# Splits of the last feed-forward operands as steps behind the first products, three weight adds on the Vector engine, and the tail's product on GpSimd

## The chip, the cores and the metric

The kernel runs on one core of a Trainium2 chip. The metric is the device time of one execution in microseconds, and the comparison is between medians of several runs. The kernel before took 2356.03 us (median of three: 2354.13, 2356.03 and 2356.07). The profile is of one further execution, which took 2354.07 us.

The engines go by the names of the profile: PE is the Tensor engine, which multiplies matrices, DVE the Vector engine, ACT the Scalar engine, POOL is GpSimd and SP the engine whose queue issues nearly all DMA transfers. Each engine works through its own list of instructions strictly in order, and waits at an instruction until what it needs is there.

## The reference

One layer of a trunk over x of 2048 rows by 1024, and a last norm. The part that the change touches begins at the output projection:

```python
x = x + merged @ w_out[l]
xn = rms_norm(x, ffn_norm_g[l])
gate, up = jnp.split(xn @ w_gate_up[l], 2, axis=-1)
x = x + (jax.nn.silu(gate) * up) @ w_down[l]
return rms_norm(x, final_norm_g)
```

with `rms_norm(x, g) = x * rsqrt(mean(x*x) + EPS) * g`. D_MODEL is 1024 and D_FF 2816. Everything ahead of that (attention with forget gates, spatial gating, their norms) fills `merged` and is the same in both kernels.

## The kernel before

**Precision.** Every float32 operand of a product is split in two: a high part rounded to the matrix format (a CAST on ACT, line 127) and the remainder, low (a subtraction on DVE, line 130). A product is three passes: high by high, high by low, low by high. So each operand of a product costs one ACT and one DVE instruction of its size before PE may use it.

**The output projection** (products at line 1190) goes row block by row block of 128 rows. When both halves of a block are added to x (line 1184, on DVE, reading the products' banks), `out_done` finishes it: ACT squares the row and sums it (1157), DVE makes mean plus EPS (`r3a`, 174), POOL takes the inverse root as a power (`r3r`, 177, in the helper `rsqrt`), DVE scales the row (`xn`, 1163), PE transposes it (1170), ACT copies the transposed tiles out (1172) and SP stores them in the DRAM buffer XT. The feed-forward reads its operand from XT.

**The feed-forward** computes each block product from 7 products of halves instead of 8, with sums and differences of the operands' quarters. The resident operand, from XT, has quarters b11, b12, b21, b22 in four large tiles `sg` (each 128 partitions by 4 by 512, so 128x2048). From these `first_operands` makes the seven resident operands of the first set: R4 = b22 - b12, R1 = t1 = b11 + b12, R3 = b22 - t1, R0 = b11, R2 = b21, R5 = b21 - t1, R6 = b22, each as a high and a low half. It is a generator, and the out-projection's loop takes steps of it in between. R5 and R6 are the last step, taken ahead of the feed-forward's loop. The subtraction for R5 is done on the whole tile, after the sum b11 + b12 has been made a second time over b11. `keep_as` writes the high and low half of an operand over tiles that are free.

The streamed operand is a weight. An `Up` item is 128 columns of gate and the same of up; its four quarters (`raw`, each 128x512) are loaded by `load` at line 1520 and combined by `stream`, which yields the seven operands one by one, each with its split `wh`, `wl`. There are four sums or differences among them. Which engine does each is read from the string `SE = 'pvpv'` (p is POOL, v DVE), through the helper `tt` at line 1433. The first, a21 + a22, is on POOL.

There are 22 Up items for each half of the rows (sets 1 and 2), then three sets of 8 `Down` items. Two items make a group, and a group has seven slots, n = 0 to 6. In the loop over slots PE multiplies the slot's operands (1743), then `evac` takes the result out of its bank: `u` is ACT's copy of the slot 0 product (1535 in Up, 1490 in Down), and the other slots add to it. The loop also calls `make`, which asks `stream` for operands some slots ahead. Each set's resident operands are made by `refill` during the last group of the set before, one in each slot.

**The tail.** The last Down item holds the last two row blocks. In its `evac` at slots 3 and 4 a half row's squares are summed (1594) and the half is multiplied by the final norm's gain (1583 and 1590, both on DVE). In `done`, when the other half is there too, it is squared, the sums joined (1605), POOL takes the root (1607), DVE scales one half by root and gain (1609) and ACT the one that has the gain already by the root alone (1611). All four halves are stored by SP (1610 and 1612).

**What sets the order.** A framework's scheduler places every instruction on its engine's list, mostly in the order of the program, with priorities and the buffers' reuse. So moving a step in the program moves instructions in each list, and the lists have to be read to see where.

Of the kernel before, what the change touches and what calls it, by code (L numbers as in the profile page):

```python
# [11 lines left out]
ALU = mybir.AluOpType  # L12
# [13 lines left out]
CH = 512  # L26
# [58 lines left out]
def trunk(ctx: ExitStack, tc: tile.TileContext, x, x_t, mix_g, w_in, b_f, ln_g, ln_b, w_st, b_st, on_g, w_out,  # L85
# [1361 lines left out]
                sg.append(fetch(s, n + 4))  # L1447
            yield r

    def stream(a11, a12, a21, a22):  # L1450

        kh = a11.shape[1]

        tt(SE[0], a21, a21, a22, ALU.add)
        yield split(a11, kh)
        tt(SE[1], a11, a21, a11, ALU.subtract)
        yield split(a11, kh)
        yield split(a12, kh)
        tt(SE[2], a12, a12, a11, ALU.subtract)
        tt(SE[3], a11, a22, a11, ALU.subtract)  # L1460
        yield split(a21, kh)
        yield split(a11, kh)
        yield split(a22, kh)
        yield split(a12, kh)
# [44 lines left out]
    class Up:  # L1509
# [12 lines left out]
            self.raw = raw  # L1522

        def start(self):
            self.ops = stream(*self.raw)

        def evac(self, n):
            ps = self.ps
# [27 lines left out]
    class Down(Rows):  # L1556
# [10 lines left out]
            self.raw = raw  # L1567

        def start(self):
            self.ops = stream(*self.raw)  # L1570

        def source(self, t):
            return XA[t]
# [1 line left out]
        def evac(self, n):  # L1575
            super().evac(n)
            if (self.kb, self.tp, n) == (2, NB // 2 - 1, 3):

                xt = self.x[0][:, 0:CH]
                self.a = T(pev, [P, 1], F32, "a5")  # L1580
                self.squares(xt, self.a)
                nc.vector.tensor_scalar(self.a, self.a, 1.0 / D, EPS, ALU.mult, ALU.add)
                nc.vector.tensor_tensor(xt, xt, finb[:, 0:CH], ALU.mult)
            if (self.kb, self.tp, n) == (2, NB // 2 - 1, 4):

                xt = self.x[1][:, CH:]
                self.b = T(pev, [P, 1], F32, "b5")
                self.squares(xt, self.b)
                nc.vector.tensor_scalar(self.b, self.b, 1.0 / D, EPS, ALU.mult, ALU.add)
                nc.vector.tensor_tensor(xt, xt, finb[:, CH:], ALU.mult)  # L1590

        def squares(self, xt, ss):
            jk = T(pev, [P, D], mybir.dt.bfloat16, "jk", bufs=1)
# [2 lines left out]
        def done(self, t, xt, at):  # L1596
            if self.kb < 2:
                ld(XA[t], xt)
                return
            ss = T(pev, [P, 1], F32, "ss4")  # L1600
            o = out[t * P : (t + 1) * P, :]
            if t >= NB - 2:
                at, by, c = (slice(CH, D), slice(0, CH), self.a) if t == NB - 2 else (slice(0, CH), slice(CH, D), self.b)
                self.squares(xt[:, at], ss)
                self.last = nc.vector.scalar_tensor_tensor(ss, ss, 1.0 / D, c, ALU.mult, ALU.add)
                r = T(pev, [P, 1], F32, "r4r")
                nc.gpsimd.tensor_tensor(r, ss, mhalf[:, 0:1], ALU.pow)
                yield
                nc.vector.scalar_tensor_tensor(xt[:, at], xt[:, at], r, finb[:, at], ALU.mult, ALU.mult)
                ld(o[:, at], xt[:, at])  # L1610
                nc.scalar.activation(xt[:, by], xt[:, by], AF.Copy, scale=r)
                ld(o[:, by], xt[:, by])
                return
            while now[0] == at:
                yield
            with behind(*copies):
                self.squares(xt, ss)
            yield
            r = rsqrt(pev, ss, 1.0 / D, "r4")
            nc.vector.scalar_tensor_tensor(xt, xt, r, finb, ALU.mult, ALU.mult)  # L1620
            ld(o, xt)
            yield
# [43 lines left out]
    def first_operands():  # L1666
# [2 lines left out]
        for i in range(4):  # L1669
            yield  # L1670

        def halves(a, src, t=None, add=None):
            R[a] = resident(a)
            for i in range(2):
                o = slice(2 * i, 2 * i + 2)
                u = t[i] if t else src[:, o]
                if add:
                    tt("v", u, add[0][:, o] if add[0] is not t else u, add[1][:, o] if add[1] is not t else u, add[2])
                hi_of(nc.scalar, R[a][0][:, o], u)
                yield  # L1680
                lo_of(nc.vector, R[a][1][:, o], u, R[a][0][:, o])
                yield

        yield from halves(4, b12, add=(b22, b12, ALU.subtract))
        t1 = [raw4().rearrange("p (a b) t -> p a (b t)", a=2) for _ in range(2)]
        yield from halves(1, None, t1, (b11, b12, ALU.add))
        yield from halves(3, None, t1, (b22, t1, ALU.subtract))
        yield "wait"
        R[0] = keep_as(0, b11)
        R[2] = keep_as(2, b21)  # L1690
        yield "wait"
        with behind(E["sq"], E["xn"]):
            tt("v", b11, b11, b12, ALU.add)
            tt("v", b21, b21, b11, ALU.subtract)
            R[5] = keep_as(5, b21)
            R[6] = keep_as(6, b22)
        yield "wait"

    fo = first_operands()
    m, at = 0, None  # L1700
    for _ in og:
# [3 lines left out]
        if E["t"] == NB - 2 and E["half"] == 0 and not loaded:  # L1705
# [2 lines left out]
            next(fo)  # L1708
            load(0)
            make()  # L1710
    next(fo)
    make()
    load(1)
    nextR = [None] * 7
# [2 lines left out]
    for q in range(len(slots)):  # L1717
# [9 lines left out]
        last = last and s < 5  # L1727
        if n == 0 and last:
            fill = refill(s + 1, sg)
        while nq < len(slots) and len(made) + len(grp[slots[nq][0]][2]) <= LW:  # L1730
            make()
        if n == 0:
# [16 lines left out]
        for m in () if late and n == 0 else (0, 1) if late and n == 1 else (n,):  # L1749
            for it in its:  # L1750
                it.evac(m)
        if n == 0:
            now[0] = p
        tail = p == len(grp) - 1
# [4 lines left out]
        if tail and n == 6:  # L1759
            next(posts[1])  # L1760
            with behind(its[0].last):
                next(posts.pop(0), None)
        if last:
            nextR[n] = next(fill)
        if sums and p:
            try:
                sums.send((n, p))
# [48 lines left out]
```

## Time and profile before

| What | us |
|---|---|
| median of three runs | 2356.03 |
| the profiled execution | 2354.07 |
| its span, first to last instruction | 2352.4 |
| PE busy in the span | 2325.9 (99%) |
| DVE, ACT, POOL busy | 1681.5, 1059.0, 607.6 |
| PE waiting for xn (line 1163), three times | 4.1 |
| PE waiting for a weight's low half (130) in the feed-forward, twice | 1.7 |
| PE waiting for the copy u, in Up and in Down, once each | 1.0 and 1.0 |

The span starts with the first instruction and times in it are counted from there; 1.7 us of the execution lie outside it. PE works without pause but for short waits, so whatever time the kernel can lose or gain shows as a gap between two of PE's instructions or as time after its last one. The out-projection ends and the feed-forward begins at about 1077 us, the down projection begins at about 1900 us, and PE's last product ends at about 2343 us.

### The profile page before, as it was taken

To read this page: it belongs to the slowest core of one execution; us is meant where nothing else is said; L and a number is where in the kernel's file an instruction comes from. 1 tells how busy PE (TensorE), PEld (TensorE's weight loads), DVE (VectorE), ACT (ScalarE), POOL (GpSimd) and SP (SyncE) were. 2 spreads that over 40 slices of the span, in tenths; PEclk is the share of its full clock that TensorE was granted. 3 is DMA by queue.
4 is the path that set the end of the run, shared out by engine and by line. 5 is a ranking of instruction groups with operands and counts; after the bars stand their busy time and mean duration, and the time that the engine had idled before them with its cause. 6 is when DMAs were issued, how large, how long until landed. Compare 5 with 4: busy or idle time off the path is not lost.

```text
span 2352.4 us, 31826 instructions
## 1 busy us (share of the span) xinstructions
PE 2325.9 (99%) x10566; PEld 1889.8 (80%) x10566; DVE 1681.5 (71%) x2783; ACT 1059.0 (45%) x1774; POOL 607.6 (26%) x704
## 2 busy tenths in 40 slices
PE   9999999999999999999999999999999999999998
PEld 7778777777787778877888888888888878888886
DVE  6658668888888677576565666866666686685788
ACT  5322137767788786344323233532333352332433
POOL 1100011121121232131222323232323235343431
PEclk9999999999999999999999999999999999999999
DMA  8845668656677785773445444724444355564554
GB/s 270 296 158 190 210 185 213 179 160 174 175 216 245 223 244 163 230 225 117 125 126 176 139 150 127 241 76 140 129 140 144 90 196 190 191 250 170 194 193 150
DMA packets 375948, 423.90 MB, mean 180 GB/s; under 512 B 23956, under 2 KB 277588, under 8 KB 371816
## 3 DMA queue, kind: packets, MB, share of 16 engines
q1 hardware_dynamic: 359800, 378.62, 52.2%
q0 software_dynamic: 7616, 27.33, 3.4%
q10 hardware_dynamic: 8368, 15.91, 1.9%
q8 instruction: 85, 1.39, 0.3%
q14 instruction: 79, 0.65, 0.1%
HBM read 280.87 MB, written 140.91 MB: 179 GB/s over the span
## 4 chain that ended last, share of the span: by engine, by line
PE 72%; DVE 4%; DMA 2%; issue 2%; ACT 1%; POOL 0%; SPq 0%; POOLq 0%; DVEq 0%; ACTq 0%
PE pp L1743 51%; PE z L930 5%; PE pp L1190 2%; PE oz L1190 2%; PE tp L774 2%; PE tp L769 2%; PE mx_ps L737 2%; PE mx_ps L736 2%; PE tp L771 1%; PE mx_ps L361 1%; DVE wl L130 1%; PE z L971 1%; DVE raw L1433 0%; DMA sg<-XT 0%; DVE Pl L130 0%
## 5 line engine op out<-in xcount | busy, mean ns | idle before, releaser
L127 ACT CAST wh<-raw 128x512 fp32r<-128x512 f32 (+2 forms) x492 | 304.5, 621 | 741.1 <-PE pp L1743 640.6
L130 DVE TENSOR_TENSOR wl<-raw,wh 128x512 fp32r<-128x512 f32 (+2 forms) x496 | 370.9, 755 | 26.9 <-ACT wh L127 26.7
L1743 PE MATMUL pp<-wl,wh 128*128 128x512 f32 x1056 | 325.5, 389 | 2.1 <-ACT u L1535 1.0
L1743 PE MATMUL pp<-wh,wh 128*128 128x512 f32 x1056 | 325.2, 389 | 0.0
L1433 POOL TENSOR_TENSOR raw<-raw 128x512 f32<-128x512 f32 (+1 forms) x124 | 170.5, 1376 | 572.8 <-DMA raw<-in_w_gu_dram 311.2
L130 DVE TENSOR_TENSOR Pl<-Pt,Ph 128x512 fp32r<-128x512 f32 (+1 forms) x320 | 194.3, 614 | 75.3 <-ACT Ph L127 68.4
L1743 PEld LDWEIGHTS pp<-wl,wh 128*128 128x128 f32 x1056 | 198.0, 188 | 44.4 <-ACT u L1535 1.4
L1743 PEld LDWEIGHTS pp<-wh,wh 128*128 128x128 f32 x1056 | 198.1, 188 | 41.2
L739 ACT ACTIVATE Pt<-mx_ps 128x512 f32<-128x512 f32 (+1 forms) x320 | 168.7, 533 | 113.4 <-PE mx_ps L737 94.8
L1743 PE MATMUL pp<-wh,wl 128*128 128x512 f32 x528 | 205.4, 389 | 0.0
L1743 PE MATMUL pp<-wl,wl 128*128 128x512 f32 x528 | 205.4, 389 | 0.0
L1433 DVE TENSOR_TENSOR raw<-raw,raw 128x512 f32<-128x512 f32 (+1 forms) x112 | 136.5, 1219 | 90.2 <-POOL raw L1433 87.4
L930 PE MATMUL z<-wh,xz 128*128 128x512 f32 x496 | 187.3, 396 | 0.0
L127 ACT CAST Ph<-Pt 128x512 fp32r<-128x512 f32 (+1 forms) x320 | 175.7, 557 | 14.6 <-DMA ST<-zvh 0.9
L363 DVE TENSOR_REDUCE mx<-mx_ps 128x1 f32<-128x512 f32 x192 | 130.3, 684 | 19.9 <-PE mx_ps L361 19.0
L749 POOL TENSOR_SCALAR_AFFINE_SELECT Ph<-Ph 128x128 fp32r<-128x128 f32 x128 | 49.7, 388 | 293.8 <-DVE Pl L130 200.8
L361 PE MATMUL mx_ps<-D,A 66*128 66x512 f32 (+2 forms) x320 | 118.5, 374 | 2.6 <-DVE mx L366 1.6
L736 PE MATMUL mx_ps<-A,D 74*128 74x512 f32 (+1 forms) x320 | 117.9, 369 | 0.8 <-ACT Pt L739 0.7
L774 PE MATMUL tp<-Pl,V 128*128 128x512 f32 (+1 forms) x320 | 117.6, 368 | 0.8 <-POOL Pl L749 0.3
L769 PE MATMUL tp<-Ph,V 128*128 128x512 f32 (+1 forms) x320 | 117.2, 366 | 0.6 <-POOL Ph L749 0.5
L737 PE MATMUL mx_ps<-B,C 128*128 128x512 f32 (+1 forms) x320 | 117.3, 367 | 0.0
L1743 PEld LDWEIGHTS pp<-wl,wl 128*128 128x128 f32 x528 | 99.1, 188 | 20.6
(354 smaller groups left out, 5281.4 us busy)
## 6 DMA issues: line engine op xcount, KB each, us to landing
raw<-in_w_gu_dram SPq DMA_DIRECT2D x88, 512.0 KB
xz<-XS SPq DMA_DIRECT2D x31, 1024.0 KB
HD<-hT SPq DMA_DIRECT2D x44, 512.0 KB
SM<-xa SPq DMA_DIRECT2D x30, 512.0 KB
D<-KH SPq DMA_DIRECT2D x112, 128.0 KB
XA<-xa SPq DMA_DIRECT2D x27, 512.0 KB
sg<-SM SPq DMA_DIRECT2D x12, 1024.0 KB
raw<-HD SPq DMA_DIRECT2D x24, 512.0 KB
```

What stands on the lines that cost most here:

```text
L127: return nc.scalar.copy(o, i) if eng is nc.scalar else eng.tensor_copy(o, i)
L130: return eng.tensor_tensor(o, i, f(h), ALU.subtract)
L361: last_mx.append(nc.tensor.matmul(pm[:, 0:n], lhs, Dt[0 : lhs.shape[0], 0:n], start=True, stop=True))
L363: nc.vector.tensor_reduce(mx[:, a, s : s + 1], pm, AX.X, ALU.max)
L736: nc.tensor.matmul(st[:, off:], Dt[:, b * P : (b + 1) * P], A[:, off:], start=True, stop=False)
L737: nc.tensor.matmul(st[:, off:], C[:, b * P : (b + 1) * P], B[:, off:], start=False, stop=True)
L739: nc.scalar.activation(Pt[:, off:], st[:, off:], AF.Exp)
L769: nc.tensor.matmul(pv[:, off:], V[:, 0:P], Ph[:, off:], start=kb == 0, stop=False)
L774: nc.tensor.matmul(pv[:, off:], V[:, 0:P], Pl[:, off:], start=False, stop=kb == 4 * j + 3)
L930: nc.tensor.matmul(pz, xz[a][:, k, :], w[b][:, k, :], start=n == 0, stop=n == 3 * KT - 1)
L1433: return (nc.vector if e == "v" else nc.gpsimd).tensor_tensor(o, a, b, op)
L1743: nc.tensor.matmul(pm, a[:, k, :], b[:, k, :], start=on is None and k == 0 and e == 0, stop=k == it.kh - 1 and e == 2, skip_group_check=n ...
```

## The change

The change has four parts.

First, in Up items of the first half with fi below 2, the sum a21 + a22 is done on DVE and not on POOL.

Second, the source of R5 is made half by half together with R1: `halves` takes a new argument, and while t1's half is in hand it also does b12 = b21 - t1 for that half (128x1024 each). So b11 + b12 is not made a second time. The splits of R5 and R6 become two steps, taken in the feed-forward's loop after the products of slots 1 and 2 of the first group.

Third, for the set that follows the second Up set, the steps for R5 and R6 are taken at slots 0 and 2 of the new set's first group and not in the last group of the old one.

Fourth, in the tail, the multiplication by the gain at line 1590 is done on POOL, and the stores at line 1612 are issued by ACT.

```diff
-    def stream(a11, a12, a21, a22):
+    def stream(a11, a12, a21, a22, e="p"):
         kh = a11.shape[1]
-        tt(SE[0], a21, a21, a22, ALU.add)
+        tt(e, a21, a21, a22, ALU.add)
         yield split(a11, kh)
...
         def start(self):
-            self.ops = stream(*self.raw)
+            self.ops = stream(*self.raw, "v" if not self.half and self.fi < 2 else SE[0])
...
         def start(self):
-            self.ops = stream(*self.raw)
+            self.ops = stream(*self.raw, SE[0])
...
                 nc.vector.tensor_scalar(self.b, self.b, 1.0 / D, EPS, ALU.mult, ALU.add)
-                nc.vector.tensor_tensor(xt, xt, finb[:, CH:], ALU.mult)
+                nc.gpsimd.tensor_tensor(xt, xt, finb[:, CH:], ALU.mult)
...
                 nc.scalar.activation(xt[:, by], xt[:, by], AF.Copy, scale=r)
-                ld(o[:, by], xt[:, by])
+                nc.scalar.dma_start(o[:, by], xt[:, by])
...
-        def halves(a, src, t=None, add=None):
+        def halves(a, src, t=None, add=None, rest=None):
...
                 lo_of(nc.vector, R[a][1][:, o], u, R[a][0][:, o])
+                if rest:
+                    tt("v", rest[0][:, o], rest[1][:, o], u, ALU.subtract)
                 yield
...
-        yield from halves(1, None, t1, (b11, b12, ALU.add))
+        yield from halves(1, None, t1, (b11, b12, ALU.add), (b12, b21))
...
-        with behind(E["sq"], E["xn"]):
-            tt("v", b11, b11, b12, ALU.add)
-            tt("v", b21, b21, b11, ALU.subtract)
-            R[5] = keep_as(5, b21)
-            R[6] = keep_as(6, b22)
-        yield "wait"
+        for i, src in ((5, b12), (6, b22)):
+            with behind(E["sq"], E["xn"]):
+                R[i] = keep_as(i, src)
+            yield "wait"
...
-    next(fo)
     make()
     load(1)
...
+            over = [5, 6] if s == 2 else []
...
+        if p == 0 and n in (1, 2):
+            next(fo)
...
-        if last:
+        if last and n not in over:
             nextR[n] = next(fill)
+        if s == 3 and i == 0 and n in (0, 2):
+            R[over.pop(0)] = next(fill)
```

Three places show how the lists move. A row is line, operation, output<-inputs and the tile's size; the numbers in the names tell buffers apart and differ a little between the two kernels.

**POOL, at the end of the out-projection, before.** `raw_3186` and `raw_12165` are the sums a21 + a22 of the first two Up items, `r3r` and `rar` roots of rows, `rd` row sums.

```order
L177 TENSOR_TENSOR rar_11876<-raa_11874,mhalf_206 128x1
L1433 TENSOR_TENSOR raw_3186_12161<-raw_3186_12161 128x512
L177 TENSOR_TENSOR r3r_11859<-r3a_11857,mhalf_206 128x1
L1100 TENSOR_TENSOR rd_11842<-rd_11842 128x256
L1101 TENSOR_TENSOR rd_11842<-rd_11842 128x128
L1433 TENSOR_TENSOR raw_12165<-raw_12165 128x512
L177 TENSOR_TENSOR r3r_11981<-r3a_11979,mhalf_206 128x1
```

The same piece of DVE in the changed kernel; `R3l` is the low half of R3, `wl` a weight's low half, `xn` a scaled row.

```order
L174 TENSOR_SCALAR raa_11875<-tp_11862 128x1
L130 TENSOR_TENSOR R3l_11941<-raw_3104_11775,R3h_11940 128x1024
L174 TENSOR_SCALAR r3a_11858<-ss_3119_11834 128x1
L1184 SCALAR_TENSOR_TENSOR xa_11674<-pp_11848,rsg_208,xa_11674 128x512
L1163 SCALAR_TENSOR_TENSOR xn_11833<-xb_11562,r3r_11860,ffb_10117 128x1024
L1184 SCALAR_TENSOR_TENSOR xa_11674<-pp_11870,rar_11877,xa_11674 128x512
L130 TENSOR_TENSOR R3l_11941<-raw_11776,R3h_11940 128x1024
L1094 TENSOR_TENSOR raw_3122_11842<-raw_3122_11842,rd_11843 128x512
L1184 SCALAR_TENSOR_TENSOR xa_11674<-pp_11891,rsg_208,xa_11674 128x512
L130 TENSOR_TENSOR wl_11960<-raw_11836,wh_11959 128x512
L1433 TENSOR_TENSOR raw_3186_12163<-raw_3186_12163 128x512
```

```order
L1184 SCALAR_TENSOR_TENSOR xa_11674<-pp_11917,rar_11877,xa_11674 128x512
L130 TENSOR_TENSOR wl_11964<-raw_3122_11842,wh_11963 128x512
L1433 TENSOR_TENSOR raw_12167<-raw_12167 128x512
L174 TENSOR_SCALAR r3a_11981<-ss_3150_11969 128x1
L174 TENSOR_SCALAR raa_11997<-tp_11986 128x1
L1163 SCALAR_TENSOR_TENSOR xn_11968<-xa_11674,r3r_11983,ffb_10117 128x1024
```

Both sums are on DVE, the first behind the row's scaling, the second just ahead of the next row's r3a; on POOL the roots follow each other. Both halves of R3's low part, which stood together ahead of the first of these rows, now stand around it.

**DVE, where the feed-forward begins.** Before; the tiles of 128x2048 belong to R5 and R6.

```order
L1163 SCALAR_TENSOR_TENSOR xb_12247<-xa_11913,r3r_12252,ffb_10117 128x1024
L1433 TENSOR_TENSOR sg_3047_11504<-sg_3047_11504,sg_3048_11505 128x2048
L130 TENSOR_TENSOR wl_12260<-sg_3050_11507,wl_12260 128x2048
L1433 TENSOR_TENSOR sg_3049_11506<-sg_3049_11506,sg_3047_11504 128x2048
L130 TENSOR_TENSOR wl_12326<-raw_3186_12161,wh_12325 128x512
L130 TENSOR_TENSOR wl_12332<-raw_12165,wh_12331 128x512
L130 TENSOR_TENSOR wl_12392<-raw_3185_12159,wh_12391 128x512
L130 TENSOR_TENSOR wl_12396<-raw_12163,wh_12395 128x512
L130 TENSOR_TENSOR wh_12257<-sg_3049_11506,wh_12257 128x2048
```

And in the changed kernel:

```order
L1163 SCALAR_TENSOR_TENSOR xb_12249<-xa_11915,r3r_12254,ffb_10117 128x1024
L130 TENSOR_TENSOR wl_12320<-raw_3186_12163,wh_12319 128x512
L130 TENSOR_TENSOR wh_12385<-sg_3048_11505,wh_12385 128x2048
L130 TENSOR_TENSOR wl_12326<-raw_12167,wh_12325 128x512
L130 TENSOR_TENSOR wl_12422<-sg_3050_11507,wl_12422 128x2048
L130 TENSOR_TENSOR wl_12389<-raw_3185_12161,wh_12388 128x512
L130 TENSOR_TENSOR wl_12393<-raw_12165,wh_12392 128x512
```

Two of the four large pieces are left, and a weight's low half stands ahead of each. On ACT at the same place the two copies u stood behind two casts of the next weights, and now behind one. From the loop's second group to the tail the lists of all engines are the same in both kernels.

**DVE and ACT in the tail.** DVE in the changed kernel, where the row of line 1590 stood between the first two rows before:

```order
L1589 TENSOR_SCALAR b_4974_22084<-b_4974_22084 128x1
L1433 TENSOR_TENSOR sg_4955_22001<-sg_4955_22001,u_22004 128x512
L1505 TENSOR_TENSOR sg_4955_22001<-sg_4955_22001,pp_22056 128x512
L1605 SCALAR_TENSOR_TENSOR ss_4977_22101<-ss_4977_22101,b_4974_22084 128x1
L1605 SCALAR_TENSOR_TENSOR ss_4980_22117<-ss_4980_22117,a_4971_22067 128x1
```

ACT in the changed kernel, whose list ended before with the second of the two rows of line 1611:

```order
L1594 ACTIVATE jk_22102,ss_4977_22101<-sg_4955_22001 128x512
L1594 ACTIVATE jk_22118,ss_4980_22117<-sg_4955_22001 128x512
L1611 ACTIVATE sg_4955_22001<-sg_4955_22001,r4r_22105 128x512
L1611 ACTIVATE sg_4955_22001<-sg_4955_22001,r4r_22121 128x512
L1612 DMA out_dram<-sg_4955_22001 128x512 x2
```

Both stores of line 1612 come after both scalings on ACT's list; before, SP issued them, the first of them ahead of the two stores of line 1610.

## The prediction

> **What bounds the kernel now.** I read the page first, then all waits of TensorE (PE), then the timeline around each of PE's gaps. A timeline row is start (us), length (us), engine, line, operation, output<-inputs, and in brackets the idle time before it and what ended that.
>
> ```profile
> PE 2325.9 (99%) x10566; PEld 1889.8 (80%) x10566; DVE 1681.5 (71%) x2783; ACT 1059.0 (45%) x1774; POOL 607.6 (26%) x704
> PE tp L1170 <- DVE xn L1163: 4.1, 3, 2.2
> PE pp L1743 <- DVE wl L130: 1.7, 2, 0.9
> PE pp L1743 <- ACT u L1535: 1.0, 1, 1.0
> PE pp L1743 <- ACT u L1490: 1.0, 1, 1.0
> ```
>
> PE is busy 99% of the span, so only its gaps can be saved, plus the tail after its last product. The wait rows give the total, the count and the longest. Of those on xn one stands ahead of everything that changes, the others at 1039.31 and 1080.38 (both shown below); those on wl at 1093.33 (below, 0.93) and in the down projection (the rest of the 1.7, 0.78), those on u at 1099.59 and in the down projection (0.97). Nothing else that PE waits for lies in code that the diff touches. So the sum has four places: the rows' roots, the start of the feed-forward, the start of the down projection, the tail.
>
> **Part 1, the rows' roots.** Both out-projection rows' chains at the first place, before:
>
> ```profile
> 1030.78 2.42 DVE L130 TENSOR_TENSOR R3l<-raw,R3h 128x1024 fp32r<-128x1024 f32 x2
> 1033.12 0.74 DVE L1184 SCALAR_TENSOR_TENSOR xb<-pp,rar,xb 128x512 f32<-128x512 f32 x1
> 1033.90 1.06 ACT L1157 ACTIVATE xn<-xb 128x1024 f32<-128x1024 f32 x1 [0.95 <-DVE xb L1184]
> 1035.11 0.14 DVE L174 TENSOR_SCALAR r3a<-ss 128x1 f32<-128x1 f32 x1
> 1036.04 1.29 POOL L1433 TENSOR_TENSOR raw<-raw 128x512 f32<-128x512 f32 x1 [0.89 <-DMA raw<-in_w_gu_dram]
> 1037.29 0.55 POOL L177 TENSOR_TENSOR r3r<-r3a,mhalf 128x1 f32<-128x1 f32 x1
> 1037.88 1.28 DVE L1163 SCALAR_TENSOR_TENSOR xn<-xb,r3r,ffb 128x1024 f32<-128x1024 f32 x1 [2.62 <-POOL r3r L177]
> 1039.31 0.63 PE L1170 MATMUL tp<-ident,xn 128*128 128x128 f32 x4 [2.16 <-DVE xn L1163]
> 1042.74 0.38 SPq L1520 DMA_DIRECT2D raw<-in_w_gu_dram  x1
> 1047.27 1.29 POOL L1433 TENSOR_TENSOR raw<-raw 128x512 f32<-128x512 f32 x1 [3.43 <-DMA raw<-in_w_gu_dram]
> 1049.10 1.28 DVE L1163 SCALAR_TENSOR_TENSOR xn<-xa,r3r,ffb 128x1024 f32<-128x1024 f32 x1 [4.16 <-POOL r3r L177]
> 1051.40 0.60 PE L1170 MATMUL tp<-ident,xn 128*128 128x128 f32 x4
> ```
>
> The root r3r was ready to run at 1035.25 but stood behind a weight add that waited for its load until 1036.04. In the new order the add is gone from GpSimd (POOL) there, and DVE does one half of R3l (2.42/2 = 1.21 us) ahead of r3a: from xb at 1033.12, 0.66 + 0.60 + 0.07 + 1.21 puts r3a at 1035.66, then r3r at about 1035.9 to 1036.5, xn 36.5 to 37.8, and the transposes at 1037.93 (0.15 after xn, as before). The gap of 2.16 falls to 0.78: a gain of 1.4 there.
>
> That gain must survive the second row's chain. There the add now stands on **DVE ahead of r3a**, so it still has to see its load land: issued at 1042.74, taken up at 1047.27, 4.5 us. SP's issue waits for the same split (wl) as before and DVE reaches it no earlier, because the second half of R3l has moved in between and a load of rd had DVE idle there; I leave 1047.27 as it is. Then 0.60 for the add, r3a, r3r 0.55, xn 1.28 with the steps of 0.1 between them: xn ends at 1050.05, the transposes can go at 1050.2. Before they ran at 1051.40 (xn's end 1050.38 plus matmuls still queued ahead of them, so with no gap). With PE 1.4 earlier they are due at 1050.0. The net gain is 1051.40 - 1050.2 = **-1.2**. Queued behind the waiting add on DVE are r3a, raa and xn of that row and then the xa evacuations; PE needs none of them before those transposes. The first weight add moved the same way, behind the wl that lets SP issue the second load; its own load goes out on SP right behind the two of rd, and has landed by then if it leaves before 1042.7 - 4.5 = 1038.2: cost 0 (up to 0.6 of DVE time, with no one on PE behind it). Bounds: -1.6 if the load lands earlier, 0 if it lands 1.2 later.
>
> The third place keeps its stall:
>
> ```profile
> 1077.11 1.30 POOL L1433 TENSOR_TENSOR raw<-raw 128x512 f32<-128x512 f32 x1 [13.89 <-DVE r3a L174]
> 1080.38 0.63 PE L1170 MATMUL tp<-ident,xn 128*128 128x128 f32 x4 [1.26 <-DVE xn L1163]
> ```
>
> In the new order this subtraction (SE[2], not the add that moved) still stands just ahead of r3r_12209 on POOL, so the gap of 1.26 at 1080.38 stays: **0** (-1.26 if r3r overtakes it).
>
> **Part 2, the first feed-forward operands.** Around the two gaps, before:
>
> ```profile
> 1088.18 2.29 DVE L130 TENSOR_TENSOR wl<-sg,wl 128x2048 fp32r<-128x2048 f32 x1
> 1092.59 2.50 DVE L130 TENSOR_TENSOR wl<-raw,wh 128x512 fp32r<-128x512 f32 x4
> 1093.33 0.50 PE L1743 MATMUL pp<-R3h,wl 128*128 128x512 f32 x1 [0.93 <-DVE wl L130]
> 1098.43 0.62 ACT L127 CAST wh<-raw 128x512 fp32r<-128x512 f32 x1 [2.10 <-PE pp L1743]
> 1098.95 1.06 ACT L1535 COPY u<-pp 128x512 f32<-128x512 f32 x2
> 1099.59 0.73 PE L1743 MATMUL pp<-wl,wh 128*128 128x512 f32 x2 [0.97 <-ACT u L1535]
> ```
>
> From 1085.98 to 1092.68 DVE did three pieces of 2.29 us (the middle one is the first row) for R5 and R6 while PE waited for the next wl, which ended at 1093.27. The new order has two of the four pieces here, each behind a wl: from 1085.98, wl 0.60, R5l 2.20, wl 0.60, R6l 2.20, and three more wl, all done by 1093.4, with the wl that PE lacked already done at 1086.7. The other two pieces became four halves inside the out-projection (part of DVE's idle time: 4.16 us before one xn alone). So the 0.93 goes. The u copies, which free the banks PE waited for, stood behind a cast that itself waited for PE until 1098.43; now they stand ahead of it and can run from about 1096.3. So the 0.97 goes: together **-1.9**. The casts of R5 and R6 on ACT cost 1.9 us each as before, under 1.95 to 2.10 of idle time. Bounds: -1.9 and -0.9 (if one of the two gaps comes back behind the R6 pieces).
>
> **Part 3, the down projection.** From the loop's start to the tail not a row on any engine differs, so its 0.78 and 0.97 stay: **0** (-1.75 if both went).
>
> **Part 4, the tail.** Before, after PE's last product:
>
> ```profile
> 2342.52 0.19 ACT L1594 ACTIVATION_READ_ACCUMULATOR jk<-sg 128x1 f32 x1
> 2342.74 0.15 DVE L1589 TENSOR_SCALAR b<-b 128x1 f32<-128x1 f32 x1 [0.24 <-ACT jk L1594]
> 2342.81 0.68 DVE L1590 TENSOR_TENSOR sg<-sg,sg 128x512 f32<-128x512 f32 x1
> 2343.41 0.68 DVE L1433 TENSOR_TENSOR sg<-sg,u 128x512 f32<-128x512 f32 x1
> 2346.58 0.33 SPq L1612 DMA_DIRECT2D out_dram<-sg  x1
> 2347.02 0.72 ACT L1611 ACTIVATE sg<-sg,r4r 128x512 f32<-128x512 f32 x1 [0.47 <-POOL r4r L1607]
> 2347.40:2350.20 2.80, 0.00 (x0) 0.00 (x0) 0.38 (x1) 0.34 (x1) 0.00 (x0) 0.64 1.00 373
> ```
>
> Without L1590 on DVE, L1433 starts 0.60 earlier, at 2342.81. But L1590 now runs on POOL, released by the same accumulator read (end 2342.71), and both read two operands from SBUF. How such a pair goes, once with POOL first and once with DVE first; and POOL's lag behind ACT (1042.16 to 1042.24, 0.08):
>
> ```profile
> 1198.39 1.28 POOL L1551 TENSOR_TENSOR hT<-hT,c 128x512 f32<-128x512 f32 x1
> 1198.46 1.76 DVE L1433 TENSOR_TENSOR raw<-raw,raw 128x512 f32<-128x512 f32 x1 [1.40 <-POOL raw L1433]
> 1081.41 0.68 DVE L1433 TENSOR_TENSOR raw<-raw,raw 128x512 f32<-128x512 f32 x1
> 1081.57 1.68 POOL L1433 TENSOR_TENSOR raw<-raw 128x512 f32<-128x512 f32 x1 [2.66 <-DVE wl L130]
> 1041.53 0.63 ACT L1098 ACTIVATE rd<-raw 128x512 f32<-128x512 f32 x1 [4.63 <-DVE raw L1094]
> 1042.24 1.07 POOL L1100 TENSOR_TENSOR rd<-rd 128x256 f32<-128x256 f32 x1 [4.40 <-PE pp L1190]
> ```
>
> With POOL first, DVE's end is POOL's end plus 0.55 (1199.67, 1200.22); with DVE first it is untouched and POOL ends 1.16 late. Here POOL would start at 2342.71 + 0.08 = 2342.79, DVE at 2342.81: **POOL first by 0.02**, which is close. Then L1433 ends at 2342.79 + 1.29 + 0.55 = 2344.63 instead of 2344.09: +0.54, and the squares, both roots and the scalings behind it follow. If DVE is first: -0.60. I take POOL first, for about two cases in three.
>
> The Trainium skill ("SBUF — State Buffer", "Who interferes with whom") says that a two-SBUF-input DVE instruction contends with a GpSimd instruction that reads SBUF for a port pair that is an exclusive lock; it speaks against this move. If DVE then did its full 0.68 behind the lock, L1433 would end at 2344.76 and the term be an estimated +0.67 and the sum -2.0. The rows show 0.55 behind POOL's end, and the rows are used.
>
> The stores: four of 256 KB ran back to back from 2347.40 to 2350.20 (share of DMA 1.00), 0.70 each, the first 0.82 after its issue. In the new order both L1612 are issued by ACT behind its second scaling, so not before 2347.74. The first store is now L1610's, 2347.40 to 2348.10; the other three start at 2347.74 + 0.82 = 2348.56 and end 2.10 later, at 2350.66: **+0.46** (bounds 0, if ACT's issue starts sooner by the hole, and +0.8).
>
> The sum: -1.2 - 1.9 + 0 + 0 + 0.54 + 0.46 = **-2.1**. On the profiled execution of 2354.07 (span 2352.4 and 1.7 outside) that is 2352.0; on the median of the runs, 2356.03, it is 2353.9, since those lie at two levels (2354.13; 2356.03 and 2356.07). I predict the middle, 2352.9.
>
> **The rivals.** (a) DVE first in the tail: -0.60 for +0.54, so -3.2: 2350.8 to 2352.8. For it: 0.02 us decides; against it: the lag of 0.08. (b) The stated aims all hold, with the gaps 1.26, 0.78 and 0.97 gone too, and L1590 free: -1.4 - 1.9 - 3.0 - 0.6 = -6.9, 2347.2 to 2349.1. Against it: the order keeps what stands ahead of those products. (c) The second load lands 1.2 later (5.7 us), part 1 is 0 and the sum -0.9: 2353.2 to 2355.1. For it: loads vary, and the transfers around are moved on SP's queue. (d) Slower: the load's landing on DVE. Once the second transposes are late by the 1.2 us of part 1, every further us stalls PE one for one, since xn, the evacuations and the splits all stand behind the add on DVE. Later loads took as long as this:
>
> ```profile
> 1097.96 2.26 SPq L1520 DMA_DIRECT2D raw<-in_w_gu_dram  x2
> 1104.31 1.29 POOL L1433 TENSOR_TENSOR raw<-raw 128x512 f32<-128x512 f32 x1 [19.56 <-DMA raw<-in_w_gu_dram]
> ```
>
> At 6.3 us part 1 is +0.6 and the sum -0.3; it is slower from 6.6 us on. At twice 4.5 the sum is +2.4, 2356.5 to 2358.4; no row near it shows so late a landing, and 0.2% slower would take 11.3 us.
>
> **How the numbers follow.** Chances: my forecast 0.50, (a) 0.24, (b) 0.08, (c) 0.11, (d) 0.07. What a measurement of this kernel can tell from no change is about 0.2%, 4.7 us, so 2351.3 to 2360.7 is the same. Forecast and (c) lie inside; (a) lies across the lower edge on the lower of the two levels, (b) beyond it. A median on the lower level would also bring the forecast near the edge. (d) passes the upper edge only at its far end. That makes faster 0.28, same 0.68, slower 0.04. The range takes in the forecast, (a) and (c): 2350.0 to 2355.4.
>
> **What would show it.** Right: no weight add on POOL ahead of the first two roots, PE's gap at the first transposes 0.5 to 1.0, DVE waiting for the load of raw before r3a until about 1047.3, no gap on wl or u between 1085 and 1100, the 1.26 and the two down-projection gaps as they were; in the tail L1433 at 1.8 us under L1590 on POOL at 1.29, and a hole of about 0.46 between the first store and the other three. Wrong: L1433 at 0.68, a gap in front of the second transposes, or any gap in the feed-forward's first group.

## The result and the profile after

| | before | changed |
|---|---|---|
| median of 17 runs each, us | 2354.36 (2351.23 to 2359.02) | 2349.71 (2347.62 to 2355.25) |
| span of the profiled execution | 2352.4 | 2347.2 |

The ratio of the changed kernel to the kernel before is 0.9983, with a 95% interval of 0.9976 to 0.999: a gain of 4.0 us, 2.4 to 5.6. The forecast was a gain of 2.1. The median lies 0.3 below the range's lower end of 2350.0; the kernel before came out 1.7 lower in these runs than in the three that the forecast started from.

The page and the waits of PE in the changed kernel (total, count, longest):

```profile
PE 2324.5 (99%) x10566; PEld 1890.8 (81%) x10566; DVE 1679.4 (72%) x2784; ACT 1059.7 (45%) x1774; POOL 611.8 (26%) x703
PE tp L1170 <- DVE xn L1163: 1.3, 1, 1.3
PE pp L1743 <- ACT u L1490: 1.0, 1, 1.0
PE pp L1743 <- DVE wl L130: 1.0, 1, 1.0
```

Of three waits on xn one is left (the third place), of two on wl the one of the down projection, and the wait on u in Up is gone while the one in Down stands. The end of the out-projection in the timeline of the changed kernel, first row block and then second:

```profile
1031.11 0.74 DVE L1184 SCALAR_TENSOR_TENSOR xb<-pp,rar,xb 128x512 f32<-128x512 f32 x1
1033.57 0.14 DVE L174 TENSOR_SCALAR r3a<-ss 128x1 f32<-128x1 f32 x1
1034.03 0.55 POOL L177 TENSOR_TENSOR r3r<-r3a,mhalf 128x1 f32<-128x1 f32 x1
1034.61 1.28 DVE L1163 SCALAR_TENSOR_TENSOR xn<-xb,r3r,ffb 128x1024 f32<-128x1024 f32 x1 [0.23 <-POOL r3r L177]
1036.29 0.60 PE L1170 MATMUL tp<-ident,xn 128*128 128x128 f32 x4
1044.64 0.69 DVE L1433 TENSOR_TENSOR raw<-raw 128x512 f32<-128x512 f32 x1 [2.03 <-DMA raw<-in_w_gu_dram]
1046.06 1.28 DVE L1163 SCALAR_TENSOR_TENSOR xn<-xa,r3r,ffb 128x1024 f32<-128x1024 f32 x1 [0.60 <-POOL r3r L177]
```

PE has no gap at either place: xn ends at 1035.89, and the transposes, at 1036.29, do not wait for it. The second sum does wait for its load on DVE, as forecast, but only until 1044.64.

The start of the feed-forward:

```profile
1082.96 0.69 DVE L130 TENSOR_TENSOR wl<-raw,wh 128x512 fp32r<-128x512 f32 x1
1083.56 2.29 DVE L130 TENSOR_TENSOR wh<-sg,wh 128x2048 fp32r<-128x2048 f32 x1
1085.76 0.69 DVE L130 TENSOR_TENSOR wl<-raw,wh 128x512 fp32r<-128x512 f32 x1
1089.22 0.39 PE L1743 MATMUL pp<-R3h,wl 128*128 128x512 f32 x1
1091.99 1.07 ACT L1535 COPY u<-pp 128x512 f32<-128x512 f32 x2
```

The weight's low half is done at 1083.65, 5.6 us before PE takes it at 1089.22, and the copies u end at 1093.06 with PE going on behind them. Neither gap is left.

The tail, with the DMA share of the stores' stretch as the last row:

```profile
2337.48 1.26 POOL L1590 TENSOR_TENSOR sg<-sg,sg 128x512 f32<-128x512 f32 x1 [4.13 <-ACT jk L1594]
2337.50 1.78 DVE L1433 TENSOR_TENSOR sg<-sg,u 128x512 f32<-128x512 f32 x1
2341.80 1.53 SPq L1610 DMA_DIRECT2D out_dram<-sg  x2
2342.22 0.72 ACT L1611 ACTIVATE sg<-sg,r4r 128x512 f32<-128x512 f32 x1 [0.47 <-POOL r4r L1607]
2342.22 1.13 ACTq L1612 DMA_DIRECT2D out_dram<-sg  x2
2342.60:2345.40 2.80, 0.00 (x0) 0.00 (x0) 0.37 (x1) 0.34 (x1) 0.00 (x0) 0.50 1.00 371
```

POOL began 0.02 ahead of DVE, and line 1433 took 1.78. The stores have no hole.

**Where the time went.** PE runs the same products in both kernels, so the time between two of them can be compared from kernel to kernel. The table cuts the program at five of them (starts of PE rows, each subtracted from the next) and adds the stretch from PE's last product to the end of the span. "Again" is a second profile.

| us from ... to | before | before again | changed | adds alone, and again | operands alone | adds back |
|---|---|---|---|---|---|---|
| start to a product of line 1190 at 881.5 | 881.47 | 881.49 | 882.14 | 881.45, 884.61 | 885.57 | 883.84 |
| to the transposes at 1012.55 | 131.08 | 129.95 | 129.99 | 130.03, 130.42 | 130.03 | 129.99 |
| to those at 1039.31 (first gap) | 26.75 | 24.35 | 24.16 | 24.16, 24.16 | 24.16 | 24.16 |
| to those at 1053.23 | 13.92 | 13.93 | 13.91 | 13.91, 13.90 | 14.23 | 14.84 |
| from those at 1080.38 into the feed-forward's second group | 31.80 | 31.84 | 29.31 | 31.79, 31.78 | 29.32 | 29.32 |
| last product to end | 9.40 | 9.39 | 9.50 | 9.40, 9.38 | 9.37 | 9.52 |

The feed-forward's start is worth 2.5 in every pair. The tail costs 0.1. The rest of the 5.2 us between the first two profiles, 1.1 and 2.6 us around the out-projection's end, is not a fixed price: the kernel before, profiled again, had 3.5 of those 3.7 us without any change. The first row differs by up to 4 us between kernels whose code is the same there; it is the kernel's scatter, and it is why single profiles' spans say little.

### The profile page after: what moved, and what is told of

Read it like the earlier page. It is cut to its first block, busy times and chain, and to the rows that moved or that the text cites. A ratio compares the mean times of both kernels' runs of the same rounds, so it can differ in the third digit from the quotient of the medians.

```text
span 2347.2 us, 31824 instructions
## 1 busy us (share of the span) xinstructions
PE 2324.5 (99%) x10566; PEld 1890.8 (81%) x10566; DVE 1679.4 (72%) x2784; ACT 1059.7 (45%) x1774; POOL 611.8 (26%) x703
## 4 chain that ended last, share of the span: by engine, by line
PE 76%; DVE 3%; issue 1%; ACT 1%; DMA 0%; POOL 0%; SPq 0%; POOLq 0%; DVEq 0%; ACTq 0%
PE pp L1743 51%; PE z L930 5%; PE pp L1190 5%; PE oz L1190 2%; PE tp L774 2%; PE tp L769 2%; PE mx_ps L737 2%; PE mx_ps L736 2%; PE tp L771 1%; PE mx_ps L361 1%; PE z L971 1%; DVE wl L130 1%; PE z L1190 0%; PE tp L1170 0%; DVE Pl L130 0%
```

## The experiments

**The parts alone, and the adds undone.** e1 (and e12 below) is the kernel before with the first part alone:

```diff
-            self.ops = stream(*self.raw)
+            self.ops = stream(*self.raw, "v" if not self.half and self.fi < 2 else SE[0])
```

e2 is the kernel before with the second part alone, that is the changed `first_operands` and its two steps in the loop:

```diff
-    next(fo)
     make()
...
+        if p == 0 and n in (1, 2):
+            next(fo)
```

e3 is the changed kernel with the first part undone:

```diff
-            self.ops = stream(*self.raw, "v" if not self.half and self.fi < 2 else SE[0])
+            self.ops = stream(*self.raw, SE[0])
```

> The kernel before with the first part alone: the three weight sums a21 + a22 of the first Up items on DVE; operands, down projection and tail as before. Theory F (the forecast's): the roots were held up by the sums on POOL, and this alone gives the gain there. DVE still makes both low halves of R3 ahead of xb, so xb stays at 1033.1 and r3a at 1035.2; the sum then waits on DVE for its load until 1036.04, xn runs from about 1036.7 and PE's gap at the first transposes falls from 2.16 to about 0.9. With the second transposes on time that is -1.2 to -1.5 us. Theory R (the rival): what moved xb 2.0 us earlier in the changed kernel is the operands' part, which puts R3's low halves behind xb; then this kernel keeps a gap of 0.9 or more and gets at most half of the 2.3 us that PE gained there. Both: the gaps 0.93 and 0.97 at the feed-forward's start stay, the tail stays 9.44 us from PE's last product to the end.

> The kernel before with the second part alone: R5's source made by halves, the splits of R5 and R6 behind the first products; the weight sums on POOL, down projection and tail as before. Its list on POOL now has the first root ahead of the first sum, with no part one. Theory F: xb is set by PE, so the first transposes keep a gap of about 0.8; the second sum still stands ahead of the second root on POOL, so most of the gain there is lost; with the two gaps of the feed-forward's start gone about -1.9 to -2.5 in all. Theory R: xb comes 2.0 us earlier, PE's gap of 2.16 is gone, the loads behind it on SP go out earlier too and the second transposes have no gap: with the feed-forward's two gaps -4.5 to -5.5 us in the profile, like the whole change.

> The changed kernel with the weight sums back on POOL. Theory F: the sums cost something on POOL, a gap of 0.6 or more comes back at the first or second transposes of the out-projection: +0.6 to +1.4 against the changed kernel. Theory R: the root stands ahead of the first sum on POOL anyway, and the second load lands early enough for 1.29 us of POOL (landing 1044.6, xn until 1047.8, transposes due at 1048.4): no gap, within 0.3 us of the changed kernel in the profile up to the feed-forward.

Measured against the kernel before: e1 0.9994 (0.9985 to 1.0003), e2 0.9983 (0.9974 to 0.9992), e3 0.9981 (0.9972 to 0.999). So the operands' part alone is as fast as the whole change, within the intervals, and the adds alone bring nothing that can be told from zero. (The title and e1's expectation speak of three adds; two move: from the kernel before to e1, DVE goes from 2783 instructions to 2785 and POOL from 704 to 702.) Neither e1 nor e2 keeps a gap at the first place (24.16 in both). Theory F had expected one in both, theory R one in e1 and none in e2; its reason for that, xb brought forward by the operands' part, does not hold either, as the controls below show. In e2 the root stands ahead of the first sum on POOL's list without the sum having moved, because the operands' part changes the order around it.

The second place tells the parts apart. In e3 the sum on POOL, with its load landing at 1047.70, is ahead of the root:

```profile
1047.70 1.29 POOL L1433 TENSOR_TENSOR raw<-raw 128x512 f32<-128x512 f32 x1 [2.95 <-DMA raw<-in_w_gu_dram]
1048.95 0.55 POOL L177 TENSOR_TENSOR r3r<-r3a,mhalf 128x1 f32<-128x1 f32 x1
1050.96 0.41 PE L1170 MATMUL tp<-ident,xn 128*128 128x128 f32 x2 [0.71 <-DVE xn L1163]
```

That is 14.84 against 13.91 in the table, +0.9 (e2: +0.3), as theory F said of this place. The kernel before has no such loss there (13.92 and 13.93). So in these profiles the adds' move takes away 0.3 to 0.9 us that the operands' part alone costs at the second place, and that does not show in the medians.

**Was the gap of 2.16 the code's, or the execution's?** In e6, e7 and e9 (below) the changed kernel had gaps of 0.4 to 0.8 at 1012 and 0.4 to 0.6 at the first place; the other changed kernels had neither. What differed was the landing of a load of sg from XT: it took 10.1 to 10.3 us from its issue in these three, and 8.1 to 8.8 in the other seven. So the kernel before and the adds alone were profiled once more:

> The kernel before, unchanged, profiled a second time as a control. In its first profile PE waited 0.65 us for xn at 1012.55, because a load of sg from XT landed late, then 2.16 at 1039.31. Three of the ten changed profiles had the first gap too and then 0.4 to 0.6 at the second, the others had neither. Theory F: the sum on POOL holds the root up in any execution, so a gap of 1.0 us or more at the first transposes stays even where the load lands early; from the transposes at 1012 to those at 1039 it is 25.2 us or more (26.75 in the first profile, 24.16 in the changed kernel). Rival (the gap of 2.16 was a late load of this one execution): 24.2 to 24.6 and no gap.

> The first part alone, profiled a second time: its first profile had lost the gap of 2.16 wholly, but with an early load, and its median was only 1.0 us below the kernel before. Theory F: the sums' move alone clears the roots; without the late load 24.2 us between the two transposes, with it 24.7 to 25.5 (0.4 to 1.2 of gap left, DVE waiting for the load of raw). Theory R: with the late load it keeps 25.5 or more, since both low halves of R3 stand ahead of xb.

The kernel before, first profile:

```profile
1004.81 2.36 DVE L1433 TENSOR_TENSOR sg<-sg,sg 128x1024 f32<-128x1024 f32 x2 [4.27 <-DMA sg<-XT]
```

The changed kernel:

```profile
1003.40 2.36 DVE L1433 TENSOR_TENSOR sg<-sg,sg 128x1024 f32<-128x1024 f32 x2 [2.48 <-DMA sg<-XT]
```

The kernel before in the second profile, with the first place behind it:

```profile
1001.49 2.36 DVE L1433 TENSOR_TENSOR sg<-sg,sg 128x1024 f32<-128x1024 f32 x2 [1.26 <-DMA sg<-XT]
1029.30 0.74 DVE L1184 SCALAR_TENSOR_TENSOR xb<-pp,rar,xb 128x512 f32<-128x512 f32 x1
1032.53 1.29 POOL L1433 TENSOR_TENSOR raw<-raw 128x512 f32<-128x512 f32 x1 [1.19 <-DMA raw<-in_w_gu_dram]
1033.77 0.55 POOL L177 TENSOR_TENSOR r3r<-r3a,mhalf 128x1 f32<-128x1 f32 x1
1034.36 1.29 DVE L1163 SCALAR_TENSOR_TENSOR xn<-xb,r3r,ffb 128x1024 f32<-128x1024 f32 x1 [2.93 <-POOL r3r L177]
1035.79 0.41 PE L1170 MATMUL tp<-ident,xn 128*128 128x128 f32 x2
```

The root stands behind the sum and its load just as before, but all of it is early enough: 24.35 us between the two transposes and no gap of 0.1. The rival was right, theory F's "1.0 or more in any execution" was not. Counted from the same product (at 881.5), the addition on sg began 3.33 us later in the first profile (123.33 against 120.00), since SP issued the load 1.5 us later and it took 10.25 us instead of 8.39; the first transposes came 3.53 later (157.83 against 154.30). From that load on DVE is busy almost without a break until the roots, and hands the delay on one for one.

The second profile also settles what moved xb. In the times of the profiles xb came 2.0 us earlier in the changed kernel than in the first profile of the kernel before, and it seemed that R3's low halves, now behind xb, had made room. But counted from the start of the addition on sg, xb begins 28.3 us later in that first profile, 27.8 in the second (both with the low halves ahead of it) and 27.7 in the changed kernel; in all 14 profiles it is 27.5 to 28.3. In place of R3's halves the two half subtractions for R5 now stand ahead of xb. So xb came earlier with the load and not by the new order. What the order does shorten is the chain behind it: from xb's start to the end of xn it is 6.0 and 6.4 us in the two profiles of the kernel before, 5.0 and 5.1 with the adds alone, and 4.8 in every kernel with the operands' part.

e12 has its load at 121.62, between the two, and again 24.16, with DVE waiting for the load of raw and no gap:

```profile
1037.06 0.69 DVE L1433 TENSOR_TENSOR raw<-raw 128x512 f32<-128x512 f32 x1 [1.01 <-DMA raw<-in_w_gu_dram]
1037.67 1.28 DVE L1163 SCALAR_TENSOR_TENSOR xn<-xb,r3r,ffb 128x1024 f32<-128x1024 f32 x1
1039.19 0.38 PE L1170 MATMUL tp<-ident,xn 128*128 128x128 f32 x2
```

For the changed kernel with the load as late as in the first profile there is e6:

```profile
1004.66 2.36 DVE L1433 TENSOR_TENSOR sg<-sg,sg 128x1024 f32<-128x1024 f32 x2 [4.38 <-DMA sg<-XT]
1032.46 0.74 DVE L1184 SCALAR_TENSOR_TENSOR xb<-pp,rar,xb 128x512 f32<-128x512 f32 x1
1034.92 0.14 DVE L174 TENSOR_SCALAR r3a<-ss 128x1 f32<-128x1 f32 x1
1037.39 0.41 PE L1170 MATMUL tp<-ident,xn 128*128 128x128 f32 x2 [0.63 <-DVE xn L1163]
```

There the addition began at 123.50 and the transposes at 156.23 (in e7 at 123.50 and 155.96): 1.6 to 1.9 earlier than the 157.83 of the kernel before. So the change is worth 0.2 at the roots when the load is early, and 1.6 to 1.9 when it is late. It was late (122.8 or more) in 4 of the 14 profiles. What the adds alone do with a late load did not come up in e1 or e12 and stays open; so does why that load lands when it does.

**The tail.** In the changed kernel, e5 undoes the first of these edits, e6 the second and e4 both:

```diff
-                nc.gpsimd.tensor_tensor(xt, xt, finb[:, CH:], ALU.mult)
+                nc.vector.tensor_tensor(xt, xt, finb[:, CH:], ALU.mult)
-                nc.scalar.dma_start(o[:, by], xt[:, by])
+                ld(o[:, by], xt[:, by])
```

e7 moves the scaling ahead of the product:

```diff
-                nc.vector.tensor_scalar(self.b, self.b, 1.0 / D, EPS, ALU.mult, ALU.add)
+                nc.gpsimd.tensor_scalar(self.b, self.b, 1.0 / D, EPS, ALU.mult, ALU.add)
```

> The changed kernel with the tail as before: the product by the gain on DVE, all stores on SP. From PE's last product to the end it was 9.44 us before and 9.51 in the changed kernel. Theory (two terms that cancel: +0.46 from DVE behind POOL, about -0.4 from stores that ACT issues earlier): 9.44, so -0.07 against the changed kernel. Rival (the tail's time varies by half a us from execution to execution and the two numbers say nothing): anything from 9.0 to 9.9.

> The changed kernel with the product by the gain (line 1590) back on DVE, the stores of line 1612 left on ACT. Theory: DVE behind POOL costs 0.46, so from PE's last product to the end 9.05 instead of 9.51, with line 1433 at 0.68 and not 1.78. Rival (the four stores' transfers run back to back whoever issues them, so they set the end): 9.44.

> The changed kernel with the stores of line 1612 back on SP, the product left on POOL. Theory: ACT's earlier issue was worth 0.4, so from PE's last product to the end 9.9. Rival (the issue's place is worth nothing): 9.5.

> The changed kernel with the scaling of the sum of squares (line 1589) on POOL as well, ahead of the product. DVE then waits for nothing of ACT's there and begins line 1433 right behind line 1502, about 0.4 us before POOL can begin the product. Theory (of a pair on DVE and POOL with their operands in SBUF the later one waits): line 1433 takes 0.68, POOL's product 1.6 to 1.8, and from PE's last product to the end it is 8.1 to 8.7 instead of 9.51. Rival (the product on POOL slows DVE whoever begins): line 1433 keeps 1.5 us or more and the tail is 9.0 to 9.5.

| product on | stores on | from PE's last product to the end, us |
|---|---|---|
| DVE | SP (before, before again, e4) | 9.40, 9.39, 9.38 |
| DVE | ACT (e5) | 9.03 |
| POOL | SP (e6) | 9.84 |
| POOL | ACT (changed, e8, e9) | 9.50, 9.53, 9.94 |
| POOL, with the scaling (e7, e10) | ACT | 8.57, 8.99 |

The product on POOL costs 0.46 (9.84 - 9.38) and 0.47 (9.50 - 9.03). In the same pairs the stores on ACT save 0.35 (9.38 - 9.03) and 0.34. The two pairs of 9.5 and 9.94, and 8.57 and 8.99, are alike up to the last store's issue and differ by 0.4 in what follows it, so a single reading of this stretch is good to 0.4 only, and the stores' saving is no larger than that. In e9 it is not there (9.94 with ACT, against 9.84 with SP in e6). It does not come from the transfers. With SP issuing all stores (e6) they take the same time:

```profile
2343.60:2346.40 2.80, 0.00 (x0) 0.00 (x0) 0.36 (x1) 0.33 (x1) 0.00 (x0) 0.56 1.01 374
```

2.80 us at full share in both. That is what the Trainium skill states ("DMA: Bandwidth & Descriptors", "Issuing engines are not separate DMA queues"): the transfers run on the same 16 engines whoever issues them. What is shorter comes after them, in the program's close. In the seven profiles in which SP issues all stores, the last packet of a store ends 2.03 to 2.07 us before the program does; where ACT issues two, it is 1.64 to 1.72 in five profiles, and 2.07 and 2.12 in e9 and e10. So the saving was there five times in seven, and what decides it stays open.

The medians say nothing of terms this small. e4, e5, e6 and e7 ran at 0.998, 0.9993, 0.9986 and 0.9982 of the kernel before, each with an interval of about 0.001 (2 us) either way; e5, whose profile has a shorter tail than the changed kernel's, had the highest of the four.

In e7 DVE went first:

```profile
2338.67 0.69 DVE L1433 TENSOR_TENSOR sg<-sg,u 128x512 f32<-128x512 f32 x1
2338.94 0.47 POOL L1589 TENSOR_SCALAR b<-b 128x1 f32<-128x1 f32 x1 [4.14 <-ACT jk L1594]
2339.28 0.68 DVE L1505 TENSOR_TENSOR sg<-sg,pp 128x512 f32<-128x512 f32 x1
2339.49 1.27 POOL L1590 TENSOR_TENSOR sg<-sg,sg 128x512 f32<-128x512 f32 x1
```

Line 1433 is back at 0.69, and line 1505, which has one operand in a PE bank and overlaps POOL's product for 0.47 us, is at 0.68 as ever. This is the Trainium skill's rule ("SBUF — State Buffer", "Who interferes with whom"): a DVE instruction with two SBUF inputs and a GpSimd instruction that reads SBUF exclude each other, and one with at most one SBUF input, outside DVE's 2-port modes, is left alone. The tail's computation ends 1.6 us earlier than in the changed kernel (the last store's issue ends 4.1 us after PE's last product, against 5.7), but the end only 0.9: the four stores still need their 2.8 us. e10, which has this tail too, reads 8.99 with a close of 2.12; against e9, whose close is 2.07, it is 0.95 shorter.

**The third place and the down projection.** The two places that the change leaves as they were, mended in the changed kernel. e8 moves the third operation of the first items:

```diff
-        tt(SE[2], a12, a12, a11, ALU.subtract)
+        tt("v" if e == "v" else SE[2], a12, a12, a11, ALU.subtract)
```

e9 orders the steps for R5 and R6 behind the first products' copies and evacuation:

```diff
-            R[over.pop(0)] = next(fill)
+            with behind(copies[-1] if n == 0 else its[-1].last):
+                R[over.pop(0)] = next(fill)
```

> The changed kernel with the third weight operation of the first two Up items (a12 - a11, after which the gap of 1.26 at 1076 us is called) on DVE too. Theory: the root r3r stood behind it on POOL for 1.25 us; now it goes at once and the gap falls to 0.2 or less, and with PE's refill after a gap PE is 1.1 to 1.6 us earlier from there on. Rival (DVE does the subtraction ahead of xn and itself is late): the gap falls by 0.6 only.

> The changed kernel with the steps for R5 and R6 of the first down-projection set ordered behind the copies u (R5) and behind the evacuation of slot 2 (R6), so that the lists of ACT and DVE really change there. In the changed kernel PE's gaps there were 0.96 (wl) and 0.97 (u). Theory: the gap on wl is R6's low half of 3.4 us ahead of it on DVE, and goes; the gap on u is the cast that waits for PE ahead of the copies on ACT, which this does not move, and stays at 0.97: PE -1.0 to -1.3 from there on. Rival one (both gaps go, as at the start of the feed-forward): -2.2. Rival two (R5 or R6 now late for slots 5 and 6, or POOL keeps DVE slow): a new gap of 1 us or more, no gain.

e8 ran at 0.9973 of the kernel before (0.9962 to 0.9984). Its gap at the third transposes is 0.51, nearer the rival's size (0.6 off):

```profile
1073.49 0.69 DVE L1433 TENSOR_TENSOR raw<-raw 128x512 f32<-128x512 f32 x1
1073.66 0.93 POOL L177 TENSOR_TENSOR r3r<-r3a,mhalf 128x1 f32<-128x1 f32 x1 [14.02 <-DVE r3a L174]
1076.05 0.52 PE L1170 MATMUL tp<-ident,xn 128*128 128x128 f32 x3 [0.51 <-DVE xn L1163]
```

The root no longer stands behind a subtraction on POOL, but runs beside one on DVE that began 0.17 ahead of it, and takes 0.93 instead of 0.55: the exclusion seen from the other side. It is common in these kernels: in the kernel before, 15 of 48 roots take 0.73 to 1.53 us, each beside a DVE instruction with two SBUF inputs that began before it, and in all profiles such a root ends 0.41 to 0.42 us after that instruction. 0.75 of the 1.26 is gained.

e9 ran at 0.998 (0.9971 to 0.9989), like the changed kernel within the intervals. In the profile the gap on wl is gone and the one on u is where it was, as the theory said:

```profile
PE pp L1743 <- ACT u L1490: 1.0, 1, 1.0
1933.38 0.62 ACT L127 CAST wh<-rawd 128x512 fp32r<-128x512 f32 x1 [2.10 <-PE pp L1743]
1933.90 1.07 ACT L1490 COPY u<-pp 128x512 f32<-128x512 f32 x2
```

A cast that waits for PE until 1933.38 stands ahead of the copies that PE waits for. The stretch of PE around it is 69.26 us instead of 70.53 (1.27 less, for a gap of 0.96).

**All mended.**

> The changed kernel with the edits of the three runs on the mean on POOL, the third operation on DVE and the down projection's steps behind their first products. If the gains add, the profile is shorter than the changed kernel's by 0.8 to 1.4 in the tail, 1.1 to 1.6 at the third transposes and 1.0 to 1.3 at the down projection, 2.9 to 4.3 together: a span of 2342.9 to 2344.3, and a ratio to the kernel before of 0.9965 to 0.9970. Rival (DVE, which takes more work, gives part of it back): less than 2.5.

A ratio of 0.9971 (0.9958 to 0.9983) to the kernel before, the lowest, at a median of 2347.33 us; its interval overlaps that of the changed kernel and of e8. In its profile the single gains are all there: 0.75 at the third transposes, 1.27 at the down projection, 0.51 in the tail. That is 2.5 together, below the expected 2.9 to 4.3 and at the edge of the rival's range, since the third place and the tail gave less than expected; the span of 2346.3 is only 0.9 below the changed kernel's, because its first 881 us took 1.4 longer and the stretch up to 1012 another 0.3.

## Why the prediction was right or wrong

- **Part 1, -1.2.** Right in mechanism, mis-sized. The root did stand behind a sum that waited for its load, and the new chain was forecast well: from xb's start to the transposes 4.81 us (1033.12 to 1037.93), measured 4.93 in e6. The step that failed is taking "xb at 1033.12", and with it the gap of 2.16, as a fixed property of the order: xb was that late because a load of sg had landed late in that one execution. With the load early the kernel before loses 0.2 there, and in the changed kernel xb came at 1031.11 and the forecast gap of 0.78 did not appear. With it late, the gap was 0.63, 0.37 and 0.41 (e6, e7, e9), and the change gained 1.6 to 1.9 in e6 and e7 against the first profile. The second load, kept at 1047.27, belongs to the same execution: counted from the product at 881.5 its sum began at 165.8 there, at 162.9 in the kernel before profiled again and at 162.5 in the changed kernel.
- **The third place, 0.** Right: 1.26 in the changed kernel as before.
- **Part 2, -1.9.** Right in mechanism, mis-sized: -2.5 in all pairs (31.80 to 29.31 and so on). The gaps of 0.93 and 0.97 are measured between modelled ends: PE's products overlap, so without a gap the next row begins 0.23 after the one before, not 0.39. And the first two products after a gap come 0.34 apart instead of 0.23 (1093.33 to 1093.67 in the kernel before). So each gap removed was worth about 0.3 more than it reads. e9 shows it again: 1.27 for a gap of 0.96. One reading does not hold, without changing the sum: two half pieces and not four went into the out-projection, since the second b11 + b12 is no longer made (DVE has 2783 instructions in the kernel before and in e2).
- **Part 3, 0.** Right: 0.96 and 0.97 stand, and e9 shows that an order which does move those rows takes the first of them away.
- **Part 4, product.** Right: POOL first by 0.02, and by 0.03 in the four other profiles with this order, line 1433 at 1.78, +0.46 against the forecast 0.54. **Stores.** Wrong: forecast +0.46 for a hole behind the first store; there was no hole, and the tail was 0.35 shorter in two pairs of profiles and not shorter in e9. ACT issued its first store at 2342.22, as its second scaling began and not when it ended, so the other stores were there in time. The step that failed is "not before 2347.74", an issue taken to wait for the engine's own work ahead of it.
- **The sum, -2.1**, against -4.0 (-5.6 to -2.4) measured. With the sizes from the runs: -2.5 for part 2, +0.1 for the tail, and at the roots between -0.2 and -1.9, with 4 late loads in 14 an estimated -0.6: -3.0, inside the interval. Against these, part 1 was forecast 0.6 too large and part 2 0.6 too small, which cancel by luck; the stores' term of +0.46 is most of what is left. The two levels that the forecast saw in three runs of the kernel before are not there in 17, which lie spread from 2351.2 to 2359.0. Of the rivals, (a) and (b) did not occur, nor did (d); of (c), the load that DVE waits for, all that showed was a gap of 0.15 at the second transposes in e7.

## What to carry to other kernels

Before a gap is counted as a gain, see whether a second execution has it: here 3.5 us around two gaps came and went with one load's landing, while the 2.5 us at the feed-forward's start were the same in every profile. Before a new order is credited with bringing a step forward, count that step from an event that both kernels share and that stands ahead of the change: xb came 2.0 us earlier in the changed kernel, and yet 27.5 to 28.3 us after the same addition began in all 14 profiles. And an elementwise product moved to GpSimd costs the Vector engine its time back if both have their operands in SBUF and GpSimd starts first, be it by 0.02 us; where the move had added 0.5 us to the tail, letting the Vector engine start first took 0.9 off it.

## What was not expected of the hardware

ACT issued a DMA while its own computation was still running: its first store left at 2342.22 beside a scaling from 2342.22 to 2342.94. A power of one element per partition on GpSimd, 0.55 us alone, took 0.93 beside a subtraction on the Vector engine that had begun 0.17 us earlier. And a gap of PE cost more than it reads, by 0.3 us each here.
